# Last layer's gates over 512 tokens, divided by channels; the first three output units take channels 6 and 7 at the end of the three

## The chip, the cores and the metric

The kernel runs on one core of a Trainium2 chip. The metric is the device time of one execution in microseconds; of several runs the median is given. The engines are TensorE (PE in the rows; PEld is its weight load), VectorE (DVE), ScalarE (ACT), GpSimd (POOL) and SyncE (SP), which issues most transfers. Matrix products accumulate in PSUM, which has eight banks of 512 float32 columns by 128 partitions. A matmul of N columns streams N tokens past a 128x128 block of weights.

## The reference, cut to what matters

Two layers of a token mixer and an MLP, over 512 latent tokens (x) and 256 context tokens (xc) of 1024 channels. The last layer computes the latents only; there the context serves as keys and values.

```python
for l in range(DEPTH):                                   # DEPTH = 2
    h = modulate(rms_norm(x, norm1[l]), sh1, sc1)
    u, qs, ks, vs, q1, q2, k1, k2, vd, gl = project_streams(h @ w_in[l], ...)
    y_pool = pool_mixer(u, w_pool[l], pool_scale[l])
    y_swa  = windowed_gqa_latent(qs, ks, vs, ksc, vsc, swa_sink[l])
    y_diff = diff_head_out(diff_attention_latent(q1, q2, k1, k2, vd, k1c, k2c, vdc, lam), ...)
    # gl = sigmoid of 3 x 1024 columns of h @ w_in
    merged = gl[0] * (y_pool @ w_bp) + gl[1] * (y_swa @ w_bs) + gl[2] * (y_diff @ w_bd)
    x = x + g1 * (merged @ w_out[l])
    x = x + g2 * sq_relu_mlp(modulate(rms_norm(x, norm2[l]), sh2, sc2), w_ff1[l], w_ff2[l])
    ...   # the same for the context, but not in the last layer
```

## The kernel before, in words

Activations lie channel-major: eight tiles of 128 channels, each with the tokens along the columns. Every product is made in three matmuls, since weights and activations are split into a rounded part (hi) and the rest (lo): hi·hi, hi·lo, lo·hi. `unit_k` (lines 983 to 990) issues these three for one channel tile k; `unit` (lines 219 to 231) does so for all eight.

Weights come as one stream of tiles of 768 columns. Each is fetched into one of three raw buffers, split on ScalarE (line 170) and on VectorE or GpSimd (line 171), and lies in one of six W buffers until TensorE has used it. `blocks` fetches and splits as far as a unit needs.

**Attention.** Two groups of window attention ("swa", two heads to a step) and four heads of differential attention ("diff") run one after the other, each beside the projection z of the next group. One step is: scores S on TensorE; softmax on VectorE and ScalarE, which ends in E (line 702 for swa, 525 for diff); transposes of E on TensorE into ptr (line 715 or 535); copies of ptr into PT; the product O of PT and V. The diff heads also transpose their output ob into yt (line 564). `gate_filler` puts the 24 gate products in between: it is a generator, and each step calls it a fixed number of times. In the last layer one call is one turn, 256 tokens over all eight channel tiles (24 matmuls of 256 columns), a tanh on ScalarE and a store; two turns make a gate. The plan gives 22 of the last layer's gates to the helper, and the last two to the merge, which works on 512 columns.

In the attention PSUM is divided into four single banks, which z, ptr, tr, O, yt and the gates take in turn, and two pairs of banks for S. In the merge, the output projection and the MLP there are two single banks and three pairs.

**Output projection.** `mh` holds the merged channels, eight tiles, each made by the merge in order: hi on ScalarE (line 1305), lo on VectorE (line 1306). The output projection takes eight units m of 128 output channels, each over the eight tiles of mh, into a pair of banks; VectorE adds the result to the residual x (line 1334) and frees the pair. It goes in two turns of tokens: in layer 0 latents (512 columns) and then context, in layer 1 two halves of 256 columns. The norm for the MLP follows each turn.

**What sets the order.** A list scheduler places the instructions of each engine ahead of time, by the order in the program, by priorities (evacuations of PSUM go ahead by HIGH, line 109) and by its own estimate of when operands are there. On the chip every engine then works through its queue in that order.

Of the kernel before, what the change touches and what calls it, by code (L numbers as in the profile page):

```python
# [10 lines left out]
AF = mybir.ActivationFunctionType  # L11
# [17 lines left out]
# gates of the first branches that are worked out beside the attention of each group  # L29
# [6 lines left out]
def unit_plan(l):  # L36
    """Each layer's weights in the order of their use: (name, index, tiles of 128 rows)."""
    g = START[l]
    seq = [("swa", 0, 0)] + [("gate", j, 8) for j in range(g)]
    for i, n in enumerate(GATES_AT[l]):  # L40
        if i < 5:
            seq.append(("swa", 1, 0) if i == 0 else ("diff", i - 1, 0))
        seq += [("gate", g + j, 8) for j in range(n)]
        g += n
    tail = [x for x in seq if x[0] == "gate"][g - GATES_AT[l][5]:]
    seq = [x for x in seq if x not in tail]
    seq += [("u", m, 8) for m in range(4)] + [("wp", 0, 4)] + tail
    seq += [(name, i, 8 if name == "gate" else 4) for name, i in merge_plan(l)]
    seq += [("out", m, 8) for m in range(8)] * 2
    return seq + [(name, i, 8 if name == "ff1" else 4) for name, i, _, _ in mlp_plan(l)]  # L50


def merge_plan(l):
    """Gates that are left after the attention, and the branches."""
    g = (START[l] + sum(GATES_AT[l]))
    first = min(24, max(g, 16) + AHEAD)
    seq = [("gate", i) for i in range(g, first)]
    for i in range(24):
        if i >= 16 and first < 24:
            seq.append(("gate", first))  # L60
            first += 1
        seq.append(("br", i))
    return seq


def mlp_plan(l):
    """The MLP by parts of 512 hidden channels: (name, unit, part, turn), the first units of a part before the
    second product of the last one. The last part of the first layer goes over the latents and then the context."""
    parts = [(e, 0) for e in range(8)] + ([(7, 1)] if l == 0 else [])
    ff1 = lambda p, ms: [("ff1", 4 * p[0] + m, p[0], p[1]) for m in ms]  # L70
    seq = ff1(parts[0], range(4))
    for p, q in zip(parts, parts[1:] + [None]):
        if q:
            seq += ff1(q, range(EARLY))
        seq += [("ff2", 8 * p[0] + m, p[0], p[1]) for m in range(8)]
        if q:
            seq += ff1(q, range(EARLY, 4))
    return seq


def stream_plan(seq):
    """Columns of each tile of the stream, and where each unit's row tiles lie in it."""
    tiles, where, room = [], {}, 0
    for name, idx, nk in seq:
        if nk == 0:
            where[name, idx] = [[(len(tiles) + j, 0) for j in range(4)]]
            tiles += [CH] * 4
            room = 0
            continue
        where.setdefault((name, idx), []).append([])  # L90
        for _ in range(nk):
            if room == 0:
                tiles.append(0)
                room = CH
            where[name, idx][-1].append((len(tiles) - 1, tiles[-1]))
            tiles[-1] += 128
            room -= 128
    return tiles, where

# [34 lines left out]
class Kern:  # L134
# [26 lines left out]
    def psum(self, name, g, s):  # L161
        """The pool of the phase that begins: g single banks and s pairs of them."""
        if self.ps is not None:
            self.ps_pool.__exit__(None, None, None)
        self.ps_pool = self.tc.tile_pool(name=name, bufs=1, space=PSUM, reuse_waits="tile")
        self.ps, self.ps_bufs = self.ps_pool.__enter__(), (g, s)
# [6 lines left out]
    def rsqrt(self, out, in_, n, scale):  # L173
        """out = (in_*scale + eps) ** -0.5"""
        nc = self.nc
        t = self.sm(n, "ms")
        nc.vector.tensor_scalar(t, in_, scale, EPS, ALU.mult, ALU.add)  # L177
        nc.gpsimd.tensor_tensor(out, t, self.mhalf[:, 0:n], op=ALU.pow)  # L178

# [12 lines left out]
    def split_tile(self, eng=None):  # L192
        """Split the next tile of the weight stream into its two parts."""
        if self.pos >= len(TILES):
            return
        l, _, cols = TILES[self.pos]
        t = self.wp.tile([128, 2, CH], F32R, tag="W", name=f"W{l}")
        self.loaded[self.pos] = t
        raw = self.raw.pop(self.pos)
        self.split(t[:, 0, 0:cols], t[:, 1, 0:cols], raw[:, 0:cols], eng)  # L200
        self.pos += 1
        self.dma_tile()
# [9 lines left out]
    def blocks(self, l, name, idx, ahead=2, eng=None, turn=0):  # L212
        """The row tiles of a unit's weights as (tile, column) pairs."""
        w = [(FIRST[l] + i, o) for i, o in STREAMS[l][1][name, idx][turn]]
        self.ensure(w[-1][0] + ahead, eng)
        return [(self.loaded[i], o) for i, o in w]

# [1 line left out]
    def unit(self, ps, W, acts, groups, off=0):  # L219
        """ps[:, tokens] = sum_k W_k^T acts_k as hi*hi + hi*lo + lo*hi."""  # L220
# [13 lines left out]
    def silu2(self, out, c, t):  # L234
        """2 * silu(c)"""
        self.nc.scalar.activation(t, c, AF.Tanh, scale=0.5)
        self.nc.vector.scalar_tensor_tensor(out, t, 1.0, c, ALU.add, ALU.mult)
# [17 lines left out]
    def ada_dot(self, pool, w, c, l, j):  # L255
        """Modulation column j as a product of rows; c holds twice the vector."""
# [6 lines left out]
    def ada(self, raw, js):  # L263
        """Modulation columns, one of 128 channels at a time; the last layer's context needs only a norm."""
# [15 lines left out]
    def norm_stats(self, x, a, b):  # L280
        """The tokens' 1/rms on every partition, in PSUM."""
# [22 lines left out]
    def gains(self, l, v, j0, norm0):  # L304
        """gain * (1 + scale), for a norm whose scale starts at modulation column j0."""
# [10 lines left out]
    def modulate(self, t, h, k, a, b, gs, sh):  # L316
        """h = t * gain + shift in two parts; t is overwritten."""
# [6 lines left out]
    def norm_apply(self, x, a, b):  # L324
        """x / rms in place."""
# [31 lines left out]
    def group_w(self, l, kind, gi, eng):  # L357
        """The weights and the shape of a group."""
# [3 lines left out]
    def proj_mm(self, l, h, d, t, k0, k1):  # L362
        """Half of the projection of token tile t."""
# [207 lines left out]
    def diff_ctx(self, l, d):  # L571
        """The two context query tiles of one head, over the context keys."""
# [167 lines left out]
    def swa_ctx(self, l, d, qt):  # L740
        """One context query tile of four heads, over the context keys."""
# [151 lines left out]
    def gate_filler(self, l, h, first, last):  # L893
        """Gates in half units, kept in memory until the merge."""
        nc = self.nc
        for i in range(first, last):
            W = self.blocks(l, "gate", i, 0, nc.gpsimd)
            for (a, b) in ((0, 384), (384, 768)) if l == 0 else ((0, 256), (256, 512)):
                with self.pri("gate"):
                    ps = self.g("gate")  # L900
                    for k in range(8):
                        self.last_gate = self.unit_k(ps[:, 0:b - a], W, h, k, a, b)
                    t = self.st("tgs")
                    nc.scalar.activation(t[:, 0:b - a], ps[:, 0:b - a], AF.Tanh, scale=0.5)
                    nc.sync.dma_start(self.tgd[i][:, a:b], t[:, 0:b - a])
                yield

# [4 lines left out]
    def pool_branch(self, l, h, groups):  # L912
        """u, the pooled means and their mixing; in steps, beside other work."""
# [89 lines left out]
    def prologue(self, pl):  # L1003
        """The first layer's norm, modulation and first products, in the order that is written here."""
# [144 lines left out]
    def small(self, rows, P):  # L1149
        """Sinks, gains, lambdas and the scale of the heads' outputs."""  # L1150
# [22 lines left out]
    def run(self):  # L1173
# [48 lines left out]
        for l in range(DEPTH):  # L1222
# [13 lines left out]
            # attention  # L1236
# [15 lines left out]
            # branches and merge  # L1252
# [61 lines left out]
            # output projection, residual, MLP  # L1314
# [13 lines left out]
            for turn, (ga, gb) in enumerate(halves):  # L1328
                v = turn if l == 0 else 0
                for m in range(8):  # L1330
                    ps = self.s("out")
                    self.unit(ps, self.blocks(l, "out", m, OUTA, OUTE[turn], turn), mh, [(ga, gb)])
# [94 lines left out]
def host_arrays(inp):  # L1427
# [60 lines left out]
    # constants of the shapes alone  # L1488
# [46 lines left out]
```

## Time and profile before

| | |
|---|---|
| median of 3 runs | 2308.11 us (2307.55 to 2310.36) |
| profiled execution, first to last instruction | 2309.9 us |
| mean granted TensorE clock | 0.984 |
| TensorE busy | 2212.6 us, 12,924 matmuls |
| VectorE busy | 1502.7 us |
| ScalarE busy | 962.3 us |
| GpSimd busy | 520.8 us |
| read from memory | 233.0 MB, 112 GB/s with what is written |

The page shows no other time for the profiled execution than its span, so the span stands for it; its instructions begin at 0. Layer 0's attention and merge take the time up to some 740 us, its output projection and MLP that up to some 1350 us; the last layer's attention lies between 1394 and 1760 us, its output projection begins at 1890 us, and its MLP runs to the end. A duration of a matmul in a row is that of its pass through the array; matmuls overlap, so their pitch is the distance of two starts. The clock in a row of the windows is the share of full speed that was granted.

### The profile page before, as it was taken

The page shows a single profiled execution, that of the slowest core. Times are in us where ns is not written, and L with a number is a line of the kernel's source. Part 1 is how long each engine was busy: PE and PEld are TensorE (multiplying, and loading weights), DVE is VectorE, ACT ScalarE, POOL GpSimd, SP SyncE. Part 2 cuts the span into 40 slices and gives each one's busy share as a digit, 9 for nine tenths or more (in the row PEclk, how much of TensorE's full clock was granted, in tenths as well). Part 3 has the DMA queues.
Part 4 walks back from the last instruction along what each step waited for, and adds up shares of the span by engine and source line. Part 5 has one row for each costly group of instructions (what it writes and reads, how often), then busy time and mean ns, then how long its engine had stood idle before and what let it go on. Part 6 is the DMA issues. An engine that isn't in the chain of part 4 may idle for free.

```text
span 2309.9 us, 34112 instructions
## 1 busy us (share of the span) xinstructions
PE 2212.6 (96%) x12924; PEld 1969.0 (85%) x12924; DVE 1502.7 (65%) x2757; ACT 962.3 (42%) x1979; POOL 520.8 (23%) x525
## 2 busy tenths in 40 slices
PE   7999999989988999999999989999999999999999
PEld 2999999988876888888888879999998788888887
DVE  6667676777799776655555487766668577544443
ACT  4466655565212442222222244655556435332331
POOL 4334245432442200000000033434551122000000
PEclk9999999999998999999999989999999999999999
DMA  6222122212774543333333342212222654333332
GB/s 256 84 56 79 53 74 77 68 36 84 254 255 152 188 121 126 121 129 124 127 125 105 89 132 70 75 56 83 74 74 82 203 186 130 105 95 96 94 96 76
DMA packets 108668, 260.53 MB, mean 113 GB/s; under 512 B 13012, under 2 KB 33620, under 8 KB 107223
## 3 DMA queue, kind: packets, MB, share of 16 engines
q1 hardware_dynamic: 108502, 258.35, 35.2%
q8 instruction: 102, 1.67, 0.3%
q14 instruction: 64, 0.52, 0.1%
HBM read 233.00 MB, written 25.30 MB: 112 GB/s over the span
## 4 chain that ended last, share of the span: by engine, by line
PE 47%; issue 26%; DVE 15%; DMA 4%; ACT 4%; POOL 3%; SPq 0%; POOLq 0%; DVEq 0%; ACTq 0%
PE z L376 7%; PE ff L231 5%; PE ff L230 5%; PE ff L229 5%; PE gate L988 3%; PE gate L990 3%; PE gate L989 3%; DMA raw<-in_w_dram 2%; DMA wada<-in_wada_dram 2%; POOL W L171 2%; DVE junk L259 2%; DVE W L171 1%; ACT W L170 1%; PE ptr L715 1%; PE ada L1047 1%
## 5 line engine op out<-in xcount | busy, mean ns | idle before, releaser
L170 ACT ACTIVATE W<-raw 128x768 fp32r<-128x768 f32 (+1 forms) x383 | 320.2, 838 | 576.7 <-PE ff L231 428.2
L171 DVE TENSOR_TENSOR W<-raw,W 128x768 fp32r<-128x768 f32 x243 | 236.4, 974 | 189.4 <-ACT W L170 183.5
L376 PE MATMUL z<-W,h 128*128 128x384 f32 (+2 forms) x1728 | 313.5, 332 | 10.5 <-POOL h L1077 4.3
L171 POOL TENSOR_TENSOR W<-raw,W 128x768 fp32r<-128x768 f32 (+1 forms) x140 | 267.7, 1920 | 203.2 <-ACT W L170 199.3
L376 PEld LDWEIGHTS z<-W,h 128*128 128x128 f32 x1728 | 286.8, 191 | 14.6 <-POOL h L1077 5.1
L229 PE MATMUL ff<-h,W 128*128 128x512 f32 (+1 forms) x800 | 280.6, 351 | 1.2 <-ACT r L1350 1.2
L230 PE MATMUL ff<-h,W 128*128 128x512 f32 (+1 forms) x800 | 280.8, 351 | 0.0
L231 PE MATMUL ff<-h,W 128*128 128x512 f32 (+1 forms) x800 | 280.1, 350 | 0.0
L178 POOL TENSOR_TENSOR rs<-ms,mhalf 128x4 f32<-128x4 f32 (+4 forms) x79 | 79.7, 1009 | 867.2 <-DVE ms L177 829.0
L230 PE MATMUL ff<-f,W 128*128 128x512 f32 x736 | 264.2, 359 | 0.1
L229 PE MATMUL ff<-f,W 128*128 128x512 f32 x736 | 263.2, 358 | 0.0
L231 PE MATMUL ff<-f,W 128*128 128x512 f32 x736 | 262.4, 357 | 0.0
L259 DVE CUSTOM_DVE_ANT_0 junk<-wada,cbc,cols 128x1024 bf16<-128x1024 f32 x128 | 188.1, 1469 | 55.2 <-DMA wada<-in_wada_dram 54.4
L988 PE MATMUL gate<-h,W 128*128 128x256 f32 (+1 forms) x656 | 215.3, 328 | 6.4 <-DVE ob L554 6.4
L989 PE MATMUL gate<-h,W 128*128 128x256 f32 (+1 forms) x656 | 215.6, 329 | 0.0
L990 PE MATMUL gate<-h,W 128*128 128x256 f32 (+1 forms) x656 | 212.4, 324 | 0.0
L1380 DVE SCALAR_TENSOR_TENSOR x<-ff,mod,x 128x512 f32<-128x512 f32 (+1 forms) x192 | 121.4, 657 | 105.0 <-PE ff L231 104.8
L229 PEld LDWEIGHTS ff<-h,W 128*128 128x128 f32 x800 | 151.3, 189 | 22.9 <-ACT r L1350 1.4
L231 PEld LDWEIGHTS ff<-h,W 128*128 128x128 f32 x800 | 151.1, 189 | 21.6
L230 PEld LDWEIGHTS ff<-h,W 128*128 128x128 f32 x800 | 151.2, 189 | 21.4
L229 PEld LDWEIGHTS ff<-f,W 128*128 128x128 f32 x736 | 138.7, 189 | 21.7
L231 PEld LDWEIGHTS ff<-f,W 128*128 128x128 f32 x736 | 138.3, 188 | 21.3
(263 smaller groups left out, 4721.6 us busy)
## 6 DMA issues: line engine op xcount, KB each, us to landing
raw<-in_w_dram SPq DMA_DIRECT2D x375, 384.0 KB, 3.1
wada<-in_wada_dram SPq DMA_DIRECT2D x80, 512.0 KB, 4.1
wa<-in_wada_dram SPq DMA_DIRECT2D x8, 1024.0 KB, 8.1
tgd<-tgs SPq DMA_DIRECT2D x38, 192.0 KB, 2.3
tgl<-tgd SPq DMA_DIRECT2D x19, 384.0 KB, 4.5
tgd<-tgs SPq DMA_DIRECT2D x44, 128.0 KB, 1.9
tgl<-tgd SPq DMA_DIRECT2D x22, 256.0 KB, 4.2
yl<-yd SPq DMA_DIRECT2D x12, 384.0 KB, 3.9
```

Of the source, the lines that this page charges most:

```text
L170: nc.scalar.activation(H, src, AF.Copy)
L171: (eng or nc.vector).tensor_tensor(L, src, H.bitcast(F32), op=ALU.subtract)
L178: nc.gpsimd.tensor_tensor(out, t, self.mhalf[:, 0:n], op=ALU.pow)
L229: mm(ps[:, a:b], wh, x[0][:, r], start=k == 0, stop=False)
L230: mm(ps[:, a:b], wh, x[1][:, r], start=False, stop=False)
L231: self.last_mm = mm(ps[:, a:b], wl, x[0][:, r], start=False, stop=k == nk - 1)
L259: self.nc.vector.tensor_tensor_reduce(junk, w, c[:, v, :], 0.5, self.col(l, 21 + j), ALU.mult, ALU.add, self.mod[l][:, v, j:j + 1])
L376: self.nc.tensor.matmul(z[:, c0:384], h[k][:, hpart, ts], d["W"][k // 2][:, wpart, (k % 2) * 384 + c0:(k % 2 + 1) * 384], start=(k == 0 an ...
L988: mm(ps, wh, x[:, 0, a:b], start=k == 0, stop=False)
L989: mm(ps, wh, x[:, 1, a:b], start=False, stop=False)
L990: return mm(ps, wl, x[:, 0, a:b], start=False, stop=k == len(acts) - 1)
L1380: nc.vector.scalar_tensor_tensor(x[m][:, ga:gb], ps[:, ga:gb], self.mod[l][:, v, 40 + m:41 + m], x[m][:, ga:gb], ALU.mult, ALU.add)
```

## The change

Three things. `gate_filler`: in the last layer a call now does all 512 tokens over channel tiles 0 to 3, and the next call channel tiles 4 to 7 into the same single bank, which is held from the first call to the end of the second. The tanh and the store then follow in two pieces of 256 columns. Layer 0's turns stay 384 tokens over all channels. `out_plan`: in the first turn of the output projection the units 0, 1 and 2 go over channel tiles 0 to 5, one after the other, each in its own pair of banks; then each of the three over tiles 6 and 7; then units 3 to 7 whole. The second turn is unchanged. The rest of the diff takes out comments, so line numbers grow by 6 to 17.

```diff
+def out_plan(turn):
+    whole = [(m, 0, 8) for m in range(8)]
+    return whole if turn else [(m, 0, 6) for m in range(3)] + [(m, 6, 8) for m in range(3)] + whole[3:]
...
     def gate_filler(self, l, h, first, last):
         nc = self.nc
         for i in range(first, last):
             W = self.blocks(l, "gate", i, 0, nc.gpsimd)
-            for (a, b) in ((0, 384), (384, 768)) if l == 0 else ((0, 256), (256, 512)):
+            for turn in range(2):
+                a, b, ks = (384 * turn, 384 * turn + 384, range(8)) if l == 0 else (0, NL, range(4 * turn, 4 * turn + 4))
                 with self.pri("gate"):
-                    ps = self.g("gate")
-                    for k in range(8):
+                    if ks[0] == 0:
+                        ps = self.g("gate")
+                    for k in ks:
                         self.last_gate = self.unit_k(ps[:, 0:b - a], W, h, k, a, b)
-                    t = self.st("tgs")
-                    nc.scalar.activation(t[:, 0:b - a], ps[:, 0:b - a], AF.Tanh, scale=0.5)
-                    nc.sync.dma_start(self.tgd[i][:, a:b], t[:, 0:b - a])
+                    for c in range(a, b, 256 if l else 384) if ks[-1] == 7 else ():
+                        t = self.st("tgs")
+                        w = 256 if l else 384
+                        nc.scalar.activation(t[:, 0:w], ps[:, c - a:c - a + w], AF.Tanh, scale=0.5)
+                        nc.sync.dma_start(self.tgd[i][:, c:c + w], t[:, 0:w])
                 yield
...
-                for m in range(8):
-                    ps = self.s("out")
-                    self.unit(ps, self.blocks(l, "out", m, OUTA, OUTE[turn], turn), mh, [(ga, gb)])
+                W, pss = {}, {}
+                for m, k0, k1 in out_plan(turn):
+                    if m not in pss:
+                        pss[m], W[m] = self.s("out"), self.blocks(l, "out", m, OUTA, OUTE[turn], turn)
+                    ps = pss[m]
+                    for k in range(k0, k1):
+                        self.unit_k(ps[:, ga:gb], W[m], mh, k, ga, gb)
+                    if k1 < 8:
+                        continue
                     with tc.high_priority(offset=HIGH):
                         nc.vector.scalar_tensor_tensor(x[m][:, ga:gb], ps[:, ga:gb],
```

What this does to the order of TensorE is shown at three places. The first is the window attention of the last layer, a step of the first group: before, the end of the run of gate matmuls ahead of the first transpose of E. Twelve z matmuls, ten O matmuls and three tr transposes come first, then 16 gate matmuls, of which the last four stand here. (h_12881 and h_12882 are channel tiles 4 and 5, W_14623 is a tile of weights.)

```order
L988 MATMUL gate<-h_12881,W_14623 128x256
L989 MATMUL gate<-h_12881,W_14623 128x256
L990 MATMUL gate<-h_12881,W_14623 128x256
L988 MATMUL gate<-h_12882,W_14623 128x256
L715 MATMUL ptr<-ident,E 128x128
L989 MATMUL gate<-h_12882,W_14623 128x256
L715 MATMUL ptr<-ident,E 128x128
L990 MATMUL gate<-h_12882,W_14623 128x256
L715 MATMUL ptr<-ident,E 128x128
```

The same place in the changed kernel, from the last O matmul on:

```order
L734 MATMUL O<-PT,V 128x256
L479 MATMUL tr<-ident,rot 128x128
L483 MATMUL tr<-ident,rot 128x128 x2
L999 MATMUL gate<-h_12877,W_14498 128x512
L1000 MATMUL gate<-h_12877,W_14498 128x512
L721 MATMUL ptr<-ident,E 128x128
L1001 MATMUL gate<-h_12877,W_14498 128x512
L721 MATMUL ptr<-ident,E 128x128
L999 MATMUL gate<-h_12878,W_14498 128x512
L721 MATMUL ptr<-ident,E 128x128
```

The 16 gate matmuls of 256 columns ahead of ptr are now two of 512. In the next step of the same kind it is six; the two alternate through the windowed steps.

The second place is a diff head of the last layer, where yt is transposed. Before, a new gate begins right behind it (h_12877 is channel tile 0, h_12878 tile 1):

```order
L376 MATMUL z<-W_16141,h_12884 128x256 x3
L473 MATMUL tr<-ident,rot 128x128 x2
L564 MATMUL yt<-ident,ob 128x128
L988 MATMUL gate<-h_12877,W_16456 128x256
L989 MATMUL gate<-h_12877,W_16456 128x256
L990 MATMUL gate<-h_12877,W_16456 128x256
L988 MATMUL gate<-h_12878,W_16456 128x256
```

In the changed kernel, the same place; h_12883 and h_12884 are channel tiles 6 and 7, and the eleven gate matmuls of the turn that end here go into the bank begun in the turn before:

```order
L1001 MATMUL gate<-h_12883,W_16374 128x512
L999 MATMUL gate<-h_12884,W_16374 128x512
L1000 MATMUL gate<-h_12884,W_16374 128x512
L570 MATMUL yt<-ident,ob 128x128
L541 MATMUL ptr<-ident,E 128x128 x5
L1001 MATMUL gate<-h_12884,W_16374 128x512
L541 MATMUL ptr<-ident,E 128x128
L382 MATMUL z<-W_16535,h_12877 128x384 x3
```

The gate's turn stands ahead of yt, and the transposes of E come behind yt at once, then z.

The third place is the first turn of the output projection in layer 0 (out_8171 is the first unit, out_8202 the second; mh5 and mh6 are tiles 5 and 6 of mh). Before:

```order
L229 MATMUL out_8171<-mh5_7809,W0_8009 128x512
L230 MATMUL out_8171<-mh5_7809,W0_8009 128x512
L231 MATMUL out_8171<-mh5_7809,W0_8009 128x512
L229 MATMUL out_8171<-mh6_7810,W0_8049 128x512
L230 MATMUL out_8171<-mh6_7810,W0_8049 128x512
L231 MATMUL out_8171<-mh6_7810,W0_8049 128x512
L229 MATMUL out_8202<-mh0_7804,W0_8049 128x512
L230 MATMUL out_8202<-mh0_7804,W0_8049 128x512
L231 MATMUL out_8202<-mh0_7804,W0_8049 128x512
```

Changed (out_8195 is now the second unit, out_8219 the third); the piece is where the first unit's mh5 ends and the 36 matmuls of the second and third unit begin:

```order
L999 MATMUL out_8171<-mh5_7809,W0_8009 128x512
L1000 MATMUL out_8171<-mh5_7809,W0_8009 128x512
L1001 MATMUL out_8171<-mh5_7809,W0_8009 128x512
L999 MATMUL out_8195<-mh0_7804,W0_8049 128x512
L1000 MATMUL out_8195<-mh0_7804,W0_8049 128x512
L1001 MATMUL out_8195<-mh0_7804,W0_8049 128x512
```

The second unit begins where tile 6 of the first stood. Where the 36 end and the first unit goes on with mh6 and mh7:

```order
L999 MATMUL out_8219<-mh5_7809,W0_8196 128x512
L1000 MATMUL out_8219<-mh5_7809,W0_8196 128x512
L1001 MATMUL out_8219<-mh5_7809,W0_8196 128x512
L999 MATMUL out_8171<-mh6_7810,W0_8049 128x512
L1000 MATMUL out_8171<-mh6_7810,W0_8049 128x512
L1001 MATMUL out_8171<-mh6_7810,W0_8049 128x512
L999 MATMUL out_8171<-mh7_7811,W0_8049 128x512
L1000 MATMUL out_8171<-mh7_7811,W0_8049 128x512
L1001 MATMUL out_8171<-mh7_7811,W0_8049 128x512
```

The first unit's tiles 6 and 7 now follow the third unit's tile 5. In layer 1 the same program gives the same order, with matmuls of 256 columns. The orders of the other engines differ in few places.

## Rows read from the trace of the kernel before

**Rows 1.** The page, busy time of each engine and its share of the span.
```profile
PE 2212.6 (96%) x12924; PEld 1969.0 (85%) x12924; DVE 1502.7 (65%) x2757; ACT 962.3 (42%) x1979; POOL 520.8 (23%) x525
```

**Rows 2.** Busy time by stretch: stretch, its length, then us and instructions by engine.
```profile
1394.00:1760.00 366.00, 354.10 (x2659) 346.81 (x2660) 253.04 (x618) 214.76 (x545) 158.36 (x181) 1.00 0.26 74
2000.00:2050.00 50.00, 50.00 (x219) 40.79 (x218) 23.41 (x30) 14.87 (x20) 0.00 (x0) 1.00 0.32 97
```

**Rows 3.** Groups of lines, TensorE, 1394 to 1760 us (lines 989, 990 alike).
```profile
L988 PE MATMUL gate<-h,W 128*128 128x256 f32 x336 | 101.6, 302 | 5.2 <-DVE ob L554 5.2
```

**Rows 4.** Time line of TensorE: start, duration (pipelined), instruction.
```profile
1403.75 0.28 PE L989 MATMUL gate<-h,W 128*128 128x256 f32 x1
...
1404.95 0.28 PE L990 MATMUL gate<-h,W 128*128 128x256 f32 x1
```

**Rows 5.** Waits of TensorE in 1394 to 1760: us, times, longest.
```profile
PE gate L988 <- DVE ob L554: 5.2, 3, 1.8
...
PE ptr L715 <- DVE E L702: 2.4, 2, 1.5
```

**Rows 6.** Time line of all engines, one place in a diff head.
```profile
1634.70 0.84 ACT L170 ACTIVATE W<-raw 128x768 fp32r<-128x768 f32 x1
...
1636.56 0.34 DVE L554 SCALAR_TENSOR_TENSOR ob<-O,rc,ob 128x128 f32<-128x128 f32 x1
...
1636.95 0.38 PE L988 MATMUL gate<-h,W 128*128 128x256 f32 x1 [1.83 <-DVE ob L554]
```

**Rows 7.** Time line of all engines, two windowed steps and one diff step.
```profile
1473.23 0.28 PE L677 MATMUL S<-KK,Q 128*128 128x128 f32 x1
...
1477.53 0.55 DVE L702 TENSOR_SCALAR E<-E,rc 128x640 f32<-128x640 f32 x1
...
1478.63 0.33 PE L715 MATMUL ptr<-ident,E 128*128 128x128 f32 x1 [0.31 <-ACT zs L395]
...
1491.66 0.28 PE L677 MATMUL S<-KK,Q 128*128 128x256 f32 x1
...
1496.34 1.84 DVE L702 TENSOR_SCALAR E<-E,rc 128x512 f32<-128x512 f32 x1
...
1620.60 0.28 PE L512 MATMUL S<-KL,Q 128*128 128x256 f32 x1
...
1625.45 1.02 DVE L525 SCALAR_TENSOR_TENSOR E<-E,c 128x768 f32<-128x768 f32 x1
...
1627.35 0.27 PE L535 MATMUL ptr<-ident,E 128*128 128x128 f32 x1
```

**Rows 8.** Time line at layer 0's output projection, and one stretch of 4 us.
```profile
742.33 0.79 PE L230 MATMUL out<-mh,W 128*128 128x512 f32 x1 [4.08 <-DVE mh L1306]
...
745.14 2.54 DVE L1306 SCALAR_TENSOR_TENSOR mh<-mg,mh 128x768 fp32r<-128x768 f32 x1
...
747.74 0.79 PE L230 MATMUL out<-mh,W 128*128 128x512 f32 x1 [2.87 <-DVE mh L1306]
...
748.76 0.63 PE L229 MATMUL out<-mh,W 128*128 128x512 f32 x1
...
750.88 0.95 DVE L1306 SCALAR_TENSOR_TENSOR mh<-mg,mh 128x768 fp32r<-128x768 f32 x1
...
748.00:752.00 4.00, 4.00 (x10) 3.13 (x11) 4.00 (x7) 0.84 (x1) 0.00 (x0) 0.50 0.49 167
```

**Rows 9.** Layer 1's output projection: waits of TensorE, one stretch, VectorE's time line.
```profile
PE out L229 <- ACT mh L1305: 2.4, 1, 2.4
PE ssq L295 <- DVE acc L291: 2.3, 1, 2.3
PE out L230 <- DVE mh L1306: 0.3, 1, 0.3
...
1896.00:1900.00 4.00, 4.00 (x21) 4.00 (x22) 1.13 (x2) 1.45 (x3) 1.82 (x1) 0.59 0.92 322
...
1898.76 0.48 DVE L1334 SCALAR_TENSOR_TENSOR x<-out,mod,x 128x256 f32<-128x256 f32 x1 [2.12 <-DMA x<-xd]
```

## Prediction

> **What bounds the kernel now.** I read the engine totals first: TensorE is busy 96% of the span, VectorE 65% and ScalarE 42% [rows 1]. So time is lost where TensorE waits or issues slowly, and the views that matter are the ones that split its time. The second view, busy time by stretch, shows the stage of the first edit: in the last layer's attention, 1394 to 1760 us, TensorE is busy 354.1 of 366 us; in the MLP, 219 matmuls of 512 columns fill 50 us without a gap [rows 2]. The third, the groups of lines, gives the number of gate matmuls that the edit touches [rows 3], and the time line of TensorE their pitch [rows 4]. The waits of TensorE in that stretch then say which other engine ends last [rows 5]. For the second edit I went to the two places where the output projection begins and read time line and waits there [rows 8, 9]. All sums are made against the profiled execution's span, 2309.9 us, which is 1.8 us above the median of 2308.11; the difference is put on that median.
>
> **Wider gate matmuls.** One line of the helper runs 336 gate matmuls of 256 columns in the attention, and the helper has three such lines: 1008 there [rows 3]. At 48 to a gate that is 21 gates; the plan's 22nd runs behind the attention, 1056 in all. They become 528 of 512 columns. Starts are 0.120 us apart at 256 columns (ten steps from 1403.75 to 1404.95) [rows 4], and 50/219 = 0.2283 us at 512 columns in the MLP [rows 2]. A pair thus costs 0.240 and its replacement 0.2283 when dense; I take 0.230, since beside attention some starts follow a semaphore. 528 x 0.010 = **-5.3 us** (-6.2 at 0.2283, -2.6 if only half of it comes).
> The rows of these two pitches bear out a cost for each matmul beyond its columns. The Trainium skill, TensorE: Matmul & The Clock Gate, Back-to-back issue gap, gives N/2.4 + 2.5 ns for that gap, 109 and 216 ns here, under both measured values; by its 2.5 ns for each matmul dropped this term would be 1.3 us instead of 5.3 and the whole sum 4 us smaller, which the 0.2283 beside the 0.120 does not support.
> The tanh of each gate and its store keep their number (two pieces of 256 columns), so ScalarE and the queue of SyncE lose and gain nothing; both pieces now come together, at the end of the second turn. The weights' order is unchanged.
>
> **A wait that goes.** In three of the diff-attention heads TensorE stands before a gate, 5.2 us together [rows 5]. One starts at 1636.95 after 1.83 us of idle time: the new gate, right behind a transpose of yt, needs the bank of O, which VectorE reads last, at 1636.56, since ScalarE's part of the evacuation stood behind a weight split begun at 1634.70 [rows 6]. Now the gate at this place goes on in the bank that it already holds: eleven matmuls of it stand there, and then yt and the transposes of E. So there is no bank to wait for: **-5.2 us**. What is late next is yt's own bank, which z needs 0.9 us of matmuls later; a bad case gives back half, so -2.6 to -5.2.
>
> **A cover that shrinks.** While softmax runs on VectorE and ScalarE, TensorE works from the last score matmul S to the first transpose ptr of E. At 1473.23 S ends its run (its columns last 0.12 us more), E is done at 1477.53 + 0.55 = 1478.08, 4.7 us later, and ptr starts at 1478.63 after a stall of 0.31 [rows 7]: 5.0 us of cover, nearly all needed. Before, 16 gate matmuls of 256 columns stand in that place, 1.92 us. Now the order puts ptr after 2 or 6 of 512 columns, alternately, 0.46 or 1.38 us: the cover shrinks by 1.46 or 0.54 us. For this step that leaves 3.5 us against 4.7, a new wait of 1.2 us. At 1491.66 E takes until 1498.18, 6.4 us behind the end of S, and there only 0.6 of 7.2 us of cover goes [rows 7]: no wait. In the diff heads the step of 1620.60 has E at 1626.47 and ptr at 1627.35, 0.88 us of slack [rows 7]; it loses 1.46, and so do two like it, 0.6 each; of the nine other diff steps eight gain 0.6 of cover and one loses 0.5 of it without a wait. The same subtraction over all 16 windowed steps and these three gives ten new or longer waits, 6.8 us in sum. Some of that lateness is queueing behind work that TensorE itself releases, which moves along when TensorE waits, so I take **+5.5 us**, with +1 (the latencies follow TensorE) and +9 (none do, and the gathered tanh of 0.4 us adds to each) as ends. Behind a waiting ptr stand the gate, the next scores and z, so the wait is paid in full.
>
> **Output units that leave two channels for later.** In layer 0 TensorE waits at 742.33 for mh5 (that stays) and at 747.74 for mh6, 2.87 us, and is dense from 748.76 [rows 8]. In the new order 36 matmuls of the second and third unit over channels 0 to 5 stand behind mh5's last, which is done about 743.3. Their inputs and weights are there. They need more than 8 us, and mh6 is complete at 745.14 + 2.54, mh7 at 750.88 + 0.95 [rows 8], before TensorE comes back to them. Dense work thus begins 5.4 us earlier. Of what is done now in 743 to 749 three matmuls count as well, at the slow clock (0.50, ten starts in 4 us, 0.4 each) [rows 8], -1.3: gain **-4.1 us**, and -3 to -5 by how soon the clock comes back. Three pairs of banks are held until about 754.7; the fourth unit needs the first pair at about 757.5, so the rotation has some 2 us. Later VectorE and the transfers have slack up to the MLP, which TensorE bounds.
> In layer 1 the same place costs 2.4 us before mh7 and 0.3 before mh6 [rows 9], and 4 us from 1896 hold 21 starts where 33 would fit at 0.120, 12 x 0.12 = 1.4 us more at a clock of 0.59 [rows 9]. That is 4.1 us at most. But two things behind it come on their own time: the residual x, whose transfer VectorE awaits until 1898.76, and the norm's sum, for which TensorE waits 2.3 us afterwards [rows 9], behind weight splits that wait for transfers. If those don't move, the gain is lost there: 0 to -4.1, taken **-2.0**.
>
> **Sum.** -5.3 - 5.2 + 5.5 - 4.1 - 2.0 = -11.1 us: 2308.1 - 11.1 = **2297.0 us**.
>
> **Rivals.** (A) *The waits at ptr eat all that the gates win.* For it: steps with slack under 1 us [rows 7]. Against: eleven of the 16 windowed steps have E within 4.8 us. With the +9 end and half the bank waits given back, -5.3 - 2.6 + 9 = +1.1 in the attention, and -6.1 from the output units: 2303.1 us.
> (B) *The output units win only layer 0's part, and the gates nothing*: the last layer's start is set by transfers, and the pitch and the waits cancel. 2308.1 - 4.1 = 2304.0. For it: the wait of 2.12 for x [rows 9].
> (C) *Slower: E comes late at every windowed step.* VectorE's operations take up to three times as long in places (1.84 us for an E of 512 columns, 0.55 for one of 640) [rows 7]. If the worst latency of 6.4 us held at all 16 steps against covers of 3.3 to 6.5, TensorE would wait 26 us there, 23 more than before (2.4 on E [rows 5] and some on the banks it needs), and 4 more in the diff heads: 27 - 5.3 - 5.2 - 6.1 = +10.4, 2318.5. It decides from 16.6 us of new waits on. Against it: 5.9 us or more stands at five of the 16 steps, and the rest lie at 3.7 to 4.8.
> (D) *The held bank moves the wait instead of removing it.* A gate now keeps one of four single banks through two turns, so z, O and ptr share three. If each of the 12 diff steps waits 0.5 us for a bank, +6 takes the removed wait back: 2303. The Trainium skill, Perfetto Trace Analysis, Identifying Performance Opportunities, says that independent groups of matmuls should rotate through banks so that evacuation overlaps, which speaks for this rival; that the only bank wait of note in the trace, 5.2 us, is on a gate's new bank [rows 5] speaks against.
>
> **Chances.** Forecast 0.58 (its own range 2290 to 2302), A 0.14, B 0.12, D 0.07, C 0.09. A measurement tells 0.2%, 4.6 us, from no change: up to 2303.5 is faster, from 2312.7 slower. The forecast's cases are faster; of A and D I count two thirds faster, the rest same; B is same with a third faster; C slower, with a little same. That gives faster 0.76, same 0.16, slower 0.08. The range 2290 to 2307 takes in the forecast with both ends of its terms and A, B and D; C and a sum below -18 stay out, 0.12 together.
>
> **What would show it.** Right: 512-column gate matmuls 0.227 to 0.231 us apart; no wait of a gate on ob in the diff heads; new waits of ptr on E of 1 us in the steps with two gate matmuls before ptr, 3 to 9 us in all; TensorE dense from about 743.3 in layer 0 and no wait on mh6 or mh7 there; in layer 1 no cold stretch at 1896. Wrong: new waits of ptr over 10 us in sum; waits of z, O or yt for a bank; a wait on the norm's sum longer by what the output units won; or a wait that moves to the third unit's weights in layer 0.

## The result, and the profile after

The changed kernel takes 2326.36 us (median of 4 runs, 2324.28 to 2329.78) against 2308.53 before: ratio 1.0083, interval 1.0071 to 1.0095. It is 18 us slower; the forecast was 11 us faster. The profiled spans say the same, 2328.0 against 2309.9.

Three stretches divide the 18.1 us, read off the starts of TensorE's instructions. From the begin to the last MLP matmul of layer 0: 1367.5 us before, 1366.4 after (-1.1). From there to the last yt of the last layer's attention: 434.1 before, 458.2 after (+24.1). From there to the end: 508.2 before, 503.4 after (-4.8). So the loss lies in one stage, the attention, and it is more than the total. The first stretch lies between 1357.8 and 1367.5 in all the traces, so its -1.1 says nothing. The attention lies between 434.1 and 436.0 in the four traces whose attention is that of before, so differences of 2 us in it say nothing either.

The totals of the page [rows 1] and two stretches [rows 2]: TensorE has 528 matmuls less and is not less busy. The attention needs 389 us to do what took 366, and TensorE's busy time there rose by 4 us to 358, its idle time from 12 to 31. The MLP still starts 219 matmuls in 50 us.

```profile
PE 2215.1 (95%) x12396; PEld 1941.7 (83%) x12396; DVE 1511.5 (65%) x2757; ACT 961.3 (41%) x1979; POOL 524.9 (23%) x525
```

```profile
1393.00:1782.00 389.00, 358.00 (x2149) 319.75 (x2150) 258.06 (x616) 213.40 (x545) 158.91 (x180) 0.98 0.23 69
2030.00:2080.00 50.00, 50.00 (x219) 40.73 (x218) 23.90 (x30) 16.09 (x22) 0.00 (x0) 1.00 0.30 95
```

The gates of [rows 3] are now 168 matmuls a line, and their starts, five steps in 1.14 us, are 0.228 apart [rows 4]. The pitch came as forecast.

```profile
L999 PE MATMUL gate<-h,W 128*128 128x512 f32 x168 | 73.6, 438 | 0.0
```

```profile
1403.83 0.39 PE L1001 MATMUL gate<-h,W 128*128 128x512 f32 x1
...
1404.97 0.39 PE L1000 MATMUL gate<-h,W 128*128 128x512 f32 x1
```

The waits of TensorE in the attention, against [rows 5]: no gate waits for ob any more. In its place O waits for PT (9.0 and 3.0 us; before 1.4 and 0.2) and tr for rot (9.0 and 1.8; before 3.5, once). The wait that I had priced, ptr for E, rose from 2.4 to 3.7 us only.

```profile
PE O L557 <- DVE PT L548: 9.0, 7, 2.4
PE tr L479 <- DVE rot L468: 9.0, 4, 2.7
PE ptr L721 <- DVE E L708: 3.7, 2, 1.9
PE O L734 <- DVE PT L725: 3.0, 2, 1.7
PE z L382 <- ACT y L572: 2.7, 2, 1.4
PE tr L479 <- DVE rot L456: 1.8, 1, 1.8
```

The place of [rows 6], time line of the engines. The gate's wait is gone, and three others stand there: z waits 1.40 us for the bank of yt, and O waits twice for PT. The second PT (1652.38) stands on VectorE behind a rot of 128x256 that takes 2.01 us, and that rot begins 0.08 us behind a weight split on GpSimd (1650.37, 1.80 us) and ends 0.29 us behind it. An ob of 128x128 does the same, 1.88 us long beside the split of 1646.75.

```profile
1646.67 2.35 PE L382 MATMUL z<-W,h 128*128 128x384 f32 x12 [1.40 <-ACT y L572]
1646.75 1.85 POOL L177 TENSOR_TENSOR W<-raw,W 128x768 fp32r<-128x768 f32 x1
1646.80 1.88 DVE L568 TENSOR_SCALAR ob<-ob,rso 128x128 f32<-128x128 f32 x1 [2.60 <-POOL rso L184]
...
1649.66 0.33 PE L557 MATMUL O<-V,PT 128*128 128x128 f32 x1 [0.52 <-DVE PT L548]
...
1650.37 1.80 POOL L177 TENSOR_TENSOR W<-raw,W 128x768 fp32r<-128x768 f32 x1
1650.45 2.01 DVE L456 TENSOR_TENSOR rot<-zs,rg 128x256 f32<-128x256 f32 x1 [0.84 <-POOL rg L419]
...
1652.38 0.54 DVE L548 TENSOR_TENSOR PT<-ptr,PT 128x384 fp32r<-128x384 f32 x1
...
1652.98 0.33 PE L557 MATMUL O<-V,PT 128*128 128x128 f32 x1 [2.36 <-DVE PT L548]
```

That is no accident of one place. Of VectorE's 615 operations in the attention 23 take over 0.3 us longer than others of the same line and shape ("stretched" from here on), 30.9 us too long in sum, and all 23 lie beside a split on GpSimd. Before, it was 24 with 28.0 us: nearly as much. The groups of VectorE's lines by form in 1393 to 1782 us, of before (behind the bar us in sum and mean ns):

```profile
L434 DVE TENSOR_TENSOR xn<-zs,rg 128x256 f32<-128x256 f32 x16 | 15.4, 962 | 15.7 <-POOL rg L413 15.7
...
L461 DVE TENSOR_TENSOR rot<-rg,t 128x128 f32<-128x128 f32 x16 | 6.1, 378 | 3.1 <-POOL t L439 2.7
...
L562 DVE TENSOR_SCALAR ob<-ob,rso 128x128 f32<-128x128 f32 x13 | 3.7, 285 | 14.3 <-POOL rso L178 14.3
```

The same groups of the changed kernel:

```profile
L440 DVE TENSOR_TENSOR xn<-zs,rg 128x256 f32<-128x256 f32 x16 | 13.3, 829 | 18.3 <-POOL rg L419 18.3
...
L467 DVE TENSOR_TENSOR rot<-rg,t 128x128 f32<-128x128 f32 x16 | 9.5, 596 | 7.3 <-POOL t L445 6.8
...
L568 DVE TENSOR_SCALAR ob<-ob,rso 128x128 f32<-128x128 f32 x11 | 6.3, 574 | 10.5 <-POOL rso L184 10.5
```

Before, xn, the head of a chain with room behind it, bore the largest part (11.3 us in 9 of the 24), and rot 9.6; now xn has 8.1, rot 9.3 and ob 3.2. What moved is the place. In the windowed steps the excess fell from 19.0 to 13.2 us. In the diff heads it rose from 8.9 to 17.6, and what falls on rot and ob there from 1.9 to 12.5 (1.6 to 3.0 in the three other traces with the gates as before). Rot and ob are what TensorE's tr, yt and O stand behind: five stretched rots of the diff heads stand ahead of TensorE's five longest waits there, tr 2.5, 1.9 and 1.9 us and O 2.4 twice. The first of them:

```profile
1617.01 1.83 POOL L177 TENSOR_TENSOR W<-raw,W 128x768 fp32r<-128x768 f32 x1
1617.09 1.90 DVE L467 TENSOR_TENSOR rot<-rg,t 128x128 f32<-128x128 f32 x1 [0.78 <-POOL t L445]
...
1621.32 0.41 PE L479 MATMUL tr<-ident,rot 128*128 128x128 f32 x2 [2.47 <-DVE rot L468]
```

Besides, the new order has less left for TensorE while such an operation runs. The experiments below put a number to the two together; no run parts them. Those that read PSUM keep their time: seven copies PT of 128x512 lie beside a split and take 0.68 or 0.69 us, as without. The Trainium skill, SBUF — State Buffer, Who interferes with whom, says that a VectorE instruction with two SBUF inputs contends with a GpSimd instruction that reads SBUF, and that tensor_scalar can; the rows agree for the splits, since rot, xn and ob read SBUF alone. They do not agree for every GpSimd instruction, as the powers further below show.

The first windowed step of [rows 7] (two gate matmuls ahead of ptr): E comes 0.12 + 1475.74 to 1479.40, 3.5 us after S instead of 4.7, and ptr waits for a bank, not for E. The shorter cover was met by an earlier E.

```profile
1475.74 0.27 PE L683 MATMUL S<-KK,Q 128*128 128x128 f32 x1
...
1478.85 0.55 DVE L708 TENSOR_SCALAR E<-E,rc 128x640 f32<-128x640 f32 x1
...
1479.95 0.33 PE L721 MATMUL ptr<-ident,E 128*128 128x128 f32 x1 [0.57 <-ACT zs L401]
```

The output units of layer 0 [rows 8]: the wait at 742.49 stays, 15 matmuls start in 744 to 748, and the first turn takes 51.0 us instead of 56.3. Both turns together take 88.5 instead of 88.0. The waits show where it went: TensorE now waits 3.1 us for the norm's sum and as long as before for x, that is for VectorE, and in 785 to 825 the granted clock is 0.83 where it was 0.96. (VectorE was as busy in these stretches before: 4.0 and 32.9 us.)

```profile
744.00:748.00 4.00, 4.00 (x15) 3.25 (x14) 4.00 (x5) 0.92 (x2) 2.06 (x1) 0.75 0.30 119
785.00:825.00 40.00, 33.35 (x216) 31.52 (x214) 32.42 (x52) 18.77 (x29) 7.43 (x5) 0.83 0.32 101
```

```profile
PE out L1000 <- DVE mh L1317: 4.1, 1, 4.1
PE ssq L301 <- DVE acc L297: 3.1, 1, 3.1
PE out L999 <- DVE x L1351: 2.1, 2, 1.3
```

In layer 1 [rows 9] no wait for mh is left, the first turn is 4.1 us shorter (23.5 for 27.6), and the wait for the norm's sum grew from 2.3 to 4.6.

```profile
PE ssq L301 <- DVE acc L297: 4.6, 1, 4.6
```

### The profile page after: what moved, and what is told of

It is laid out like the page before. It is cut to its first block, busy times and chain, and to the rows that moved or that the text cites. A ratio compares the mean times of both kernels' runs of the same rounds, so it can differ in the third digit from the quotient of the medians.

```text
span 2328.0 us, 33078 instructions
## 1 busy us (share of the span) xinstructions
PE 2215.1 (95%) x12396; PEld 1941.7 (83%) x12396; DVE 1511.5 (65%) x2757; ACT 961.3 (41%) x1979; POOL 524.9 (23%) x525
## 5 line engine op out<-in xcount | busy, mean ns | idle before, releaser
L999 PE MATMUL gate<-h,W 128*128 128x384 f32 (+1 forms) x480 | 185.9, 387 | 1.1 <-DVE ob L560 1.1
L1000 PE MATMUL gate<-h,W 128*128 128x384 f32 (+1 forms) x480 | 183.2, 382 | 0.0
L1001 PE MATMUL gate<-h,W 128*128 128x384 f32 (+1 forms) x480 | 182.5, 380 | 0.0
```

The costliest lines, as they stand in the source:

```text
L999: mm(ps, wh, x[:, 0, a:b], start=k == 0, stop=False)
L1000: mm(ps, wh, x[:, 1, a:b], start=False, stop=False)
L1001: return mm(ps, wl, x[:, 0, a:b], start=False, stop=k == len(acts) - 1)
```

## The experiments

Theory O: the new order of TensorE is the loss (transposes in trains, copies late). Theory D: the held bank. Theory P, formed from the trace above: VectorE's operations stretched beside GpSimd's splits. Ratios are to the kernel before, with 95% intervals; "attention" is the stretch from layer 0's last MLP matmul to the last yt in one profile.

**Either part alone.** The output units alone (`gate_filler` as before):

> Only the output units' new order; the gates as before. Theory O (the order of TensorE in the last layer's attention is the loss, the output units gain as forecast): 4 to 6 us faster than before, ratio 0.9975 to 0.9985, no wait on mh6 or mh7 in either layer. Rival B (the output units' gain is lost again behind): within 2 us of before.

2302.8 us, 0.9980 [0.9968, 0.9992]; attention 435.3. The gates alone:

```diff
-    return whole if turn else [(m, 0, 6) for m in range(3)] + [(m, 6, 8) for m in range(3)] + whole[3:]
+    return whole
```

> Only the gates of 512 columns; the output units as before. Theory O: all of the loss is here, 22 to 24 us slower than before (2331 us). Rival (each part loses some): clearly less, 10 to 18 us slower.

2332.1, 1.0091 [1.0067, 1.0114]; attention 458.4. All of the loss is in the gates.

**Holding the bank, width as before.**

```diff
-                a, b, ks = ... if l == 0 else (0, NL, range(4 * turn, 4 * turn + 4))
+                a, b = ... if l == 0 else (256 * turn, 256 * turn + 256)
+                # ps taken in turn 0, columns 0-255 then 256-511, all eight k; tanh at the end of turn 1
```

> Gates as before in two turns of 256 columns over all channels, but both turns go into one bank, held until both tanh at the end; the output units as before. So a bank is held as long as in the changed kernel, and TensorE's order is nearly that of before. Theory O: within 5 us of before (the bank is not the loss). Rival D (one of four banks held leaves too few): 15 to 24 us slower.

2321.5, 1.0046 [1.0030, 1.0061]; attention 445.0. Between the two expectations: holding a bank costs 11 us by itself, without a wider matmul. The gate's wait on ob (5.2 us in [rows 5]) has become one of yt on ob:

```profile
PE yt L570 <- DVE ob L560: 4.3, 3, 1.5
```

**Width without holding.**

```diff
-                ... else (0, NL, range(4 * turn, 4 * turn + 4))
+                ... else (0, NL, range(8 if turn else 0, 8))
```

> Gates of 512 columns over all eight channel tiles in one call of the helper (24 matmuls), the other call empty; the output units as before. No bank is held over calls. In its order 133 transposes of E follow one another directly, against 39 before and 82 in the changed kernel. Theory O (trains of transposes leave the copies of E late for O): slower than the changed gates, 25 to 45 us over before. Rival D (holding the bank): near before or faster, -5 to +5 us.

2332.2, 1.0101 [1.0083, 1.0119]; attention 456.6. No held bank, and as slow as the change. So theory D alone doesn't explain the change. This version, though, also gathers 24 matmuls in one call, and its loss is made up differently: VectorE's stretched operations come to 16 us in its attention instead of 31, and ptr waits 9.8 us for E.

**The splits off GpSimd.** In the changed kernel, and in the one before as control:

```diff
-            W = self.blocks(l, "gate", i, 0, nc.gpsimd)
+            W = self.blocks(l, "gate", i, 0, nc.gpsimd if l == 0 else None)   # None: VectorE
```

> The changed kernel, but the second part of the gates' weight splits in the last layer runs on VectorE instead of GpSimd. TensorE's order is nearly the changed kernel's. In the trace of the changed kernel all 23 operations of VectorE that take over 0.3 us longer than their like in the last attention lie beside such a split on GpSimd. Theory P (these splits, beside rot, ob and E, make the transposes and O wait): the attention shortens by 10 us or more, 2312 to 2317 us. Theory O (the order alone): 2322 to 2328 us.

> The kernel before with the same edit of the splits alone: the control. Theory P in its strong form (the changed order brings the splits to bad places, which they had not before): within 3 us of before. If the splits cost both kernels the same: as much faster as the other is than the changed kernel.

The changed kernel falls to 2303.1, 0.9971 [0.9956, 0.9987], attention 434.9; the control to 2302.7, 0.9978 [0.9962, 0.9994], attention 429.1. One line takes 23 us off the attention of the one and 5 off that of the other, with TensorE's order there unchanged but for a few matmuls. TensorE waits nowhere in the changed kernel's attention for a split on GpSimd itself, so it isn't the splits' own time that was saved. Stretched operations of VectorE: 5 with 5.0 us, and 7 with 6.9. At the place shown above, ob and rot now take their usual time, though VectorE has the splits to do as well:

```profile
1630.20 0.28 DVE L568 TENSOR_SCALAR ob<-ob,rso 128x128 f32<-128x128 f32 x1 [2.60 <-POOL rso L184]
1630.40 0.95 DVE L177 TENSOR_TENSOR W<-raw,W 128x768 fp32r<-128x768 f32 x1
...
1633.13 0.42 DVE L456 TENSOR_TENSOR rot<-zs,rg 128x256 f32<-128x256 f32 x1 [0.84 <-POOL rg L419]
1633.47 0.55 DVE L548 TENSOR_TENSOR PT<-ptr,PT 128x384 fp32r<-128x384 f32 x1
```

The waits of TensorE in this attention: tr on rot 2.8 instead of 9.0 (0.8 instead of 6.3 in the diff heads), O on PT 2.7 instead of 9.0, z on y no shorter.

```profile
PE z L382 <- ACT y L572: 3.2, 2, 1.8
PE tr L479 <- DVE rot L468: 2.8, 4, 2.0
PE O L557 <- DVE PT L548: 2.7, 5, 0.8
```

**Slowed VectorE, or a full queue on GpSimd?** rs, rso and t run on GpSimd too, behind the splits.

```diff
+            self.nc.gpsimd.tensor_tensor(self.junk9, self.two9, t[:, 0, 0:9].bitcast(F32), op=ALU.pow)   # behind each gate split
```

> The changed kernel with the gates' splits on VectorE, and behind each a small power of 128 x 9 elements on GpSimd that takes about as long as the split took there (by the rows of line 178, 0.54 us for one column and 1.01 for four) and moves little data. It leaves GpSimd's queue as full as in the changed kernel. Theory S (VectorE is slowed beside a GpSimd instruction over large tiles): within 4 us of the version without it, 2300 to 2307 us. Theory Q (rs, rso and t of the softmax's and norms' chains stand behind the splits in GpSimd's queue): at least half of the loss comes back, 2313 to 2326 us.

2305.7, 0.9988 [0.9978, 0.9998]; attention 437.0. The 27 powers of the line below take 2.07 us on average (1.8 to 2.6), the splits took 1.85, and xn, rot and ob keep their usual time beside a power. (Two operations of VectorE beside a power are stretched; both lie beside a larger GpSimd instruction as well.) The powers read SBUF too, so the rule of the Trainium skill quoted above does not hold for every GpSimd instruction that reads there; what sets the split apart from the power, its size or something else, is not tested. 2 of the 23 us of attention come back (4 by the times, whose intervals overlap): theory S; the queue is a small part at most.

```profile
L208 POOL TENSOR_TENSOR junk<-two,W 128x9 f32<-128x9 f32 x27 | 55.9, 2072 | 27.4 <-ACT W L176 27.4
```

**Where.** 512 columns in one half of the gates, 256 in the other (`if i >= 12`, `if i < 12` ahead of the choice of columns):

> The changed kernel, but with 512-column gates only for the first 12 gates (window attention); the 10 beside and after the diff heads as before; the output units as changed. By the traces so far the windowed part is longer by 8 to 10 us and the diff heads by 14: 2310 to 2314 us. Rival (the loss is made in the diff heads alone): 2302 to 2305.

> The other half: 512-column gates only for the gates from the 13th on (diff heads); the output units as changed. 2315 to 2319 us. Rival (the loss is made in the windowed part alone): 2302 to 2305.

Windowed part alone 2307.9, 0.9996 [0.9984, 1.0009], attention 438.8; diff heads alone 2324.1, 1.0061 [1.0046, 1.0076], attention 453.9. The parts add up (4.7 + 19.8 = 24.5 of 24.1), and four fifths are made in the diff heads: more than I expected there. The stretched operations go with it: in the diff heads of the first run they come to 9.5 us, in those of the second to 17.3.

**No split on GpSimd in the attention, and the best version.** `group_w` of the last layer's diff heads on VectorE as well; the gates as before or changed. The first run has only the two edits that gained.

> The gates as before, the changed output units, and the gates' splits of the last layer on VectorE: the two edits that gained by themselves. If they add: 2308.3 - 4.6 - 5.1 = 2298 to 2300 us, and so not slower than the 512-column version with the same splits (2303.1).

> As the one before, and the diff heads' weights of the last layer are split on VectorE too, so that no split runs on GpSimd in the last attention. Theory S or Q: 0 to 3 us less again, 2296 to 2300.

> The changed kernel with no split on GpSimd in the last attention. If the collision with GpSimd was all that the 512-column gates cost, their pitch now shows: 3 to 5 us faster than the same with gates of 256 columns. If the order (copies of E late for O, banks) costs by itself: 2 to 6 us slower than it.

2298.7, 0.9958 [0.9945, 0.9970]; 2296.0, 0.9951 [0.9937, 0.9964]; and with 512 columns 2299.9, 0.9962 [0.9950, 0.9974]. These intervals overlap. Without any collision (no split runs on GpSimd there, and no operation of VectorE is stretched) the attention is still 8.8 us longer with 512 columns (431.4 against 422.6), and 6.3 us of that come back behind it (502.9 against 509.2 to the end). So no run shows the pitch to buy anything here. The second of the three beats both kernels, by 11 us and 30 us.

**The held bank without the splits.**

> Gates of 256 columns with the bank held over both turns, as in the version that was 11 us slower than before, and the gates' splits on VectorE. If the held bank costs only because the waits it moves fall beside GpSimd's splits: within 4 us of the kernel before with the same splits (2302.7). If the bank itself costs: 2309 to 2314 us.

2311.8, 1.0020 [1.0008, 1.0032]; attention 437.8 against 429.1. The bank costs 9 us with most of the collision gone too, as rival D said; the wait of yt on ob is 3.1 us there.

**Each layer's output units alone** (`out_plan(turn if l == 0 else 1)`, and the same for layer 1):

> The output units' new order in layer 0 alone, gates as before. The trace of the changed kernel has the first turn there 5.3 us shorter and the second turn's end where it was. If that gain is lost to transfers and the norm behind: 0 to 2 us faster than before. If it holds: 4 to 5 us faster.

> The same in layer 1 alone. By the two traces the first turn is 4.1 us shorter and 0.4 to 1.2 us are left at the end: 0 to 2 us faster than before. If all holds: 4 us faster.

0.9996 [0.9986, 1.0005] and 1.0009 [0.9998, 1.0020]. Neither gains beyond its interval. All the traces together show more. From the last matmul of the merge to the last of the MLP, layer 0 takes 634.7 us in the mean of the seven traces with the old order of output units and 632.8 in the ten with the new one (633.4 to 635.3 against 631.7 to 633.6). In layer 1, counting only the traces whose gates all have 256 columns, it is 416.0 in five and 414.4 in four (415.2 to 416.8 against 413.3 to 415.0).

## Why the prediction was wrong

**The pitch** was right (0.228 to 0.231 us) and so were the 528 matmuls: the attention's matmuls at their median pitches, without waits, fell by 4.5 us in sum for 5.3 forecast. In the attention it was worth nothing, since what bounds it there is not the sum of its matmuls: 431.4 us against 422.6 with no split on GpSimd either.

**The wait that goes** went, 5.2 us, and came back under other names. "So there is no bank to wait for" looked at the gate's bank alone; z then waited 2.7 us for yt's bank. That was rival D, priced at 6 and given 0.07; held banks measured 9 to 11 us with 256 columns. (The sentence of the Trainium skill that D names stands in Perfetto Trace Analysis under Optimizing Tensor Performance, Matmuls.) Why the held bank costs less with 512 columns (434.9 against 437.8, splits off GpSimd) is not settled.

**The cover that shrinks** is the step that failed. It followed one chain, S to E to ptr, and took the rest as hidden: +5.5 us on ptr, of which 1.3 appeared. In the diff heads eleven gate matmuls had moved ahead of yt and left the five transposes in a train. My order rows showed that, and I read in it only a saved bank. Behind the train PT and O had lost their cover, and ahead of it rot and tr. By pairs of neighbouring instructions, what TensorE spends above its pitch rose by 13 to 14 us between two O matmuls, some 8 from z to tr and 4 within z; from S to ptr it fell by 1.7.

**The size** comes from an interaction that no term had. Rival C named the stretched operations of VectorE, but put them at E and did not ask what stood beside them. The gates' splits beside VectorE cost the kernel before 5 us and the changed one 23 (splits moved, order kept). What the order and the bank cost without them is 6 us of attention, and 9 with the diff heads' splits moved as well. So of the 24.1 us some 15 to 18 are the collision meeting the new order, and 6 to 9 the order itself. How much of the 15 to 18 comes from rot and ob having moved beside the splits, and how much from the cover that they lost, is not shown. That this is slowing and not GpSimd's queue is shown by the powers.

**The output units** did in each first turn what was said (-5.3 for -4.1; -4.1 as the upper bound). "Later VectorE and the transfers have slack" was wrong in layer 0: VectorE was busy all of 744 to 748 and 32 of 40 us behind, and the norm's sum took the larger part of the gain. By the times they gain 4.6 us when run together, with an interval of 2 to 7, and nothing measurable when run apart; the stages of all the traces give 1.9 us in layer 0 and 1.6 in layer 1, 3.5 of the 6.1 forecast.

**The sum**: +24 in the attention instead of -5, and -6 around it. Of that -6 most is not the output units': behind the attention the gates alone have 504.3 us for the 508.2 of before, the output units alone 507.0. Why the wider gates gain there is open.

## What to carry to other kernels

When a filler moves on a busy engine, ask of each chain that it covered what is left behind: here not the softmax that I followed but the copies and rotations after it. Look up what stands beside an operation that takes three times its usual time, since a collision that is free where a chain has slack becomes the bound when a new order takes the slack away or sets another chain beside it. Moving that neighbour to another engine gained more than the wider matmul could.

## What the runs showed of the hardware

VectorE operations with two inputs in SBUF (xn, rot), and the multiplications E and ob on tiles there, ended 0.08 to 0.35 us behind the GpSimd split during which they began (rot 128x256 in 0.42 us alone, 2.01 beside it; ob 0.28 and 1.88). Those that read PSUM kept their time (PT 0.69 both ways), and so did reciprocals, whose one input lies in SBUF (0.17 us both ways). A GpSimd power of 128x9 elements, 2.07 us long on average, stretched nothing that had it alone beside it. And the splits cost less on the engine that they had delayed: 0.95 us each on VectorE against 1.85 on GpSimd.
